# One output product per token tile, and a streamed input, between two layers of a hybrid mixer

## The chip, the cores and the metric

One core of a Trainium2 chip runs the whole program. The metric is the device time of one execution in microseconds (us). The engines that matter here are TensorE (PE, matrix products and transposes into PSUM, an on-chip memory of banks), VectorE (DVE), ScalarE (ACT), GpSimd (POOL) and SyncE (SP, whose queue issues most of the loads and stores). Each engine runs its instructions strictly in its own order and waits on semaphores for the others.

## What is computed

Two layers (`DEPTH = 2`) work on 256 latent and 256 context tokens of width 1024. Each layer normalises and modulates its input, multiplies it by one wide matrix, feeds three mixers (an RWKV-7 scan in both directions, a neighbourhood attention, a differential attention), merges their gated outputs, multiplies by `w_out`, normalises, and adds the result to its input:

```python
for l in range(DEPTH):
    mod_x = jax.nn.silu(c) @ w_mod[l] + b_mod[l]          # the same for the context
    sh_x, sc_x, gt_x = jnp.split(mod_x[:, None, :], 3, axis=-1)
    hx = _rmsnorm(x, g_pre[l]) * (1.0 + sc_x) + sh_x
    hcn = _rmsnorm(hc, g_pre[l]) * (1.0 + sc_c) + sh_c
    y_x, y_c = _mixer(hx, hcn, ...)                       # ends with ... @ w_out
    x = x + gt_x * _rmsnorm(y_x, g_post[l])
    if not last:
        hc = hc + gt_c * _rmsnorm(y_c, g_post[l])
return x
```

The last layer needs only the latent tokens' output, so its queries are 256 tokens, though its keys, values and RWKV states come from all 512.

## The kernel before

**Products.** Every fp32 product is split into three: each operand becomes a rounded high part and a low rest, and `mm3` (from line 250) issues high by high, high by low and low by high. `split` (from line 223) loads a 128x512 weight tile (`wr`, 256 KB, by SP), ACT copies it to `wh`, and DVE subtracts to get `wl`. There are 6, 5 and 4 buffers of these.

**The inverse.** `rwkv_inv` inverts four families of triangular 32x32 blocks for each RWKV segment, two segments per layer, so four times in all. DVE ends it with two stream transposes of the result, `RA` and `RB`. PE multiplies the off-diagonal blocks in two rounds, `QQ` and then `EE`. ACT empties the first round (`k<-a` in the trace), which the second reads, and copies the diagonal blocks of `RA` and `RB` into `Lab` (`Lab<-X`, four copies).

**The output product.** `outproj` works through four column blocks `c` of 256 and, in each, four weight tiles `kh`. With each weight tile it visits all token tiles `t` of 128 tokens (four in layer 0, two in layer 1). Two token tiles share one PSUM tile. After a block, ACT squares each tile's product with an accumulated sum, and DVE multiplies it by the gate into `y`. `ahead` is called with each weight tile and loads the residual's rows (`xt`) and the modulation weights (`wm`, 32 tiles for the next layer, the first 16 of them by the end of the product).

**The passage.** When the whole product is done, `residual` forms one reciprocal root for all token tiles (`rsqrt`: ten small DVE operations on 128 x tiles), and then adds the scaled product to each tile's residual rows. For the next layer, `start` then normalises all four tiles (`norm_rows`, two at a time: ACT squares, a `rsqrt`, then one half of each row scaled by ACT and one by DVE), PE transposes 32 blocks of 128x128 through a PSUM tile `b` of 512 columns, ACT copies each to SBUF, DVE modulates it with `mA` and `mB`, and `split_act` makes the high and low parts `h[0]`, `h[1]` that every product of the layer reads. The modulation vectors come from `mod_rows`: four groups `g` of 32 small matmuls into PSUM `y`, a row added by DVE, one PE transpose into `z`, and `mA` by DVE and `mB` by ACT. The first products of the new layer are the column blocks 6, 2 and 4 (over 512 tokens) and block 0 (256 tokens in layer 1). The gate blocks 7 and 8 (`gates`) follow later, woven between the RWKV steps by `weave`.

**What sets the order.** A scheduler places the instructions on each engine from the program's order and from priorities. `keep_in_program_order` pins a few of them. The buffers (52 slots `k` of 128x512, 2 stages `gs`, PSUM tags `z` 3, `a` 2, `b` 2, `y` 1) decide when a tile can be written again.

Of the kernel before, what the change touches and what calls it, by code (L numbers as in the profile page):

```python
# [20 lines left out]
NX = 256  # L21
T = 512
# [112 lines left out]
class K:  # L135
# [65 lines left out]
    def rsqrt(self, v, n, scale, eps, op=ALU.add, rows=128):  # L201

        a, b, y, t = (self.small(n) for _ in range(4))
# [158 lines left out]
    def mod_rows(self, l, P, ws):  # L362
# [86 lines left out]
    def start(self, l, P, xs, mod, ws, nr=T):  # L449

        self.in_order = l == 0
# [3 lines left out]
        for _ in range(8 if l == 0 else 0):  # L455
            next(mod)
# [29 lines left out]
        r = self.now(self.z_pair(l, 0, 0, nr))  # L486
        self.have["rx", l, 0] = True
        self.have["rz", l, 0] = row[0], self.rwkv_rows(l, P, 0, 1, r, 0, nr, nr == T) or [None, None], row[1]
# [288 lines left out]
    def rwkv_inv(self, e):  # L777
# [169 lines left out]
    def gates(self, l, n, b):  # L947

        for g in range(2):
# [322 lines left out]
    def outproj(self, l, s, ns, ss, ahead):  # L1272

        G = [self.gate_rows(l, st) for st in range(ns)]
        y = []
        for t in range(2 * ns):
            yt = self.k4.tile([128, 2, 512], F32, tag="k4", name=f"y{self.count()}")
            y.append([yt[:, 0, :], yt[:, 1, :]])
        for c in range(4):
            p = [self.ps("za"[c % 2], (128, 2, 256)) for _ in range(ns)]  # L1280
# [192 lines left out]
```

## Time and profile before

| | us |
|---|---|
| median of 3 runs | 1433.27 (1431.86 to 1433.6) |
| the profiled execution | 1431.83 |
| its span | 1430.0 |
| PE busy | 1314.2 (92%) |
| DVE busy | 973.4 (68%) |
| ACT busy | 811.5 (57%) |
| POOL busy | 234.6 (16%) |

The span is what the profiler sees from the first to the last instruction, and 1.83 us lie around it. The mean granted TensorE clock was 0.964 of full speed. In the rows below, `start, length, engine, line, operation, out<-in, shape, count` stand in a timeline, and the bracket at the end says how long the engine was idle just before and which instruction or transfer ended that. A line can be that of a helper: L195 is any matmul, L199 any transpose by PE, L164 any ACT operation, L185 any `tensor_tensor`, L167 any load or store.

### The profile page before, as it was taken

Reading aid. Unit: us, or ns where it says so; the run is one execution under the profiler, and the core shown is the slowest. Engines: PE = TensorE matmul, PEld = TensorE weight load, DVE = VectorE, ACT = ScalarE, POOL = GpSimd, SP = SyncE. Lnnn points to the kernel's source line nnn. Section 1 sums busy time; section 2 is a strip of 40 time slices with the busy share of each in tenths; the row PEclk is TensorE's granted clock in tenths of the full one; section 3 lists DMA queues with packets and bytes.
Section 4 is the critical chain, followed back from the end, with each engine's and each line's share of the span. In section 5 each row is a group of like instructions: output and inputs, shape, how many; then the busy total and the mean of one; then the engine's idle time right before and its main releaser. Section 6 shows DMA issues by size and latency. Waiting matters only on the chain. (4 is left out here: it accounts for less than half of the span.)

```text
span 1430.0 us, 28585 instructions
## 1 busy us (share of the span) xinstructions
PE 1314.2 (92%) x10784; PEld 1097.1 (77%) x10784; DVE 973.4 (68%) x2047; ACT 811.5 (57%) x1750; POOL 234.6 (16%) x292
## 2 busy tenths in 40 slices
PE   6998999899998999999899969998999999989796
PEld 4865777788777876677778958887888789867686
DVE  4763469726887367768675367768837892689886
ACT  5462375545964436667533355766558736567653
POOL 0010011003110012223235001011111000022441
PEclk9999999999998999999999989999989999999998
DMA  9466642324314268422533943553613242685454
GB/s 357 125 202 191 201 137 81 118 77 143 124 62 124 64 172 236 150 97 81 199 127 122 315 156 107 186 173 115 188 61 97 75 140 69 196 266 169 130 163 148
DMA packets 112986, 212.42 MB, mean 149 GB/s; under 512 B 13088, under 2 KB 24880, under 8 KB 112848
## 3 DMA queue, kind: packets, MB, share of 16 engines
q1 hardware_dynamic: 102896, 178.33, 39.4%
q0 software_dynamic: 9952, 32.26, 6.8%
q8 instruction: 85, 1.39, 0.4%
q14 instruction: 53, 0.43, 0.1%
HBM read 176.70 MB, written 33.83 MB: 147 GB/s over the span
## 5 line engine op out<-in xcount | busy, mean ns | idle before, releaser
L195 PE MATMUL z<-k,wh 128*128 128x512 f32 (+1 forms) x2288 | 633.5, 360 | 9.5 <-ACT wh L164 5.7
L195 PEld LDWEIGHTS z<-k,wh 128*128 128x128 f32 x2288 | 406.3, 194 | 75.7 <-issue 9.4
L195 PE MATMUL z<-k,wl 128*128 128x512 f32 (+1 forms) x1144 | 408.2, 359 | 8.6 <-DVE wl L185 8.6
L164 ACT ACTIVATE wh<-wr 128x512 fp32r<-128x512 f32 x376 | 234.2, 630 | 296.8 <-PE z L195 175.9
L185 DVE TENSOR_TENSOR wl<-wr,wh 128x512 fp32r<-128x512 f32 x376 | 280.3, 752 | 170.6 <-PE z L195 70.8
L195 PEld LDWEIGHTS z<-k,wl 128*128 128x128 f32 x1144 | 221.2, 194 | 41.8 <-DVE wl L185 12.8
L195 PE MATMUL z<-wh,k 128*128 128x256 f32 x704 | 140.3, 293 | 1.5 <-ACT k L164 1.3
L195 PEld LDWEIGHTS z<-wh,k 128*128 128x128 f32 x704 | 115.5, 198 | 3.5 <-ACT k L164 1.5
L185 POOL TENSOR_TENSOR k<-k,k 64x512 fp32r<-64x512 f32 (+3 forms) x64 | 78.4, 1231 | 168.5 <-ACT k L164 88.3
L195 PE MATMUL z<-wl,k 128*128 128x256 f32 x352 | 102.7, 292 | 1.6 <-DVE wl L185 1.5
L164 ACT ACTIVATE gs<-z 128x512 f32<-128x512 f32 (+1 forms) x132 | 66.1, 501 | 63.7 <-PE z L195 54.1
L164 ACT ACTIVATE k<-k 64x256 fp32r<-64x256 f32 (+5 forms) x154 | 79.4, 541 | 29.7 <-POOL k L185 21.8
L185 DVE TENSOR_TENSOR k<-k,k 128x256 f32<-128x256 f32 (+5 forms) x126 | 79.5, 644 | 17.8 <-ACT k L164 14.6
L199 PE MATMUL b<-cst,k 128*128 128x128 f32 x384 | 67.5, 292 | 21.0 <-ACT k L164 4.8
L199 PEld LDWEIGHTS b<-cst,k 128*128 128x128 f32 x384 | 45.2, 147 | 42.5 <-issue 14.0
L164 ACT ACTIVATE k<-a,s 128x512 f32<-128x512 f32 (+1 forms) x96 | 59.1, 616 | 32.5 <-DVE s L179 31.9
L164 ACT ACTIVATE k<-b 128x256 f32<-128x256 f32 (+1 forms) x152 | 67.3, 471 | 16.9 <-PE b L199 16.0
L195 PE MATMUL a<-k,k 128*128 128x512 f32 (+1 forms) x192 | 61.0, 399 | 12.5 <-ACT k L164 10.2
L195 PEld LDWEIGHTS z<-wl,k 128*128 128x128 f32 x352 | 69.6, 198 | 2.8 <-DVE wl L185 2.3
L195 PE MATMUL a<-ar,bk 64*128 64x128 f32 (+1 forms) x512 | 49.9, 285 | 10.0 <-ACT Lab L164 9.3
L195 PEld LDWEIGHTS a<-ar,bk 64*128 64x128 f32 x512 | 42.4, 187 | 21.7 <-ACT Lab L164 16.3
L179 DVE TENSOR_REDUCE s<-a 128x1 f32<-128x512 f32 (+1 forms) x96 | 56.4, 587 | 1.7 <-PE a L195 1.7
(169 smaller groups left out, 1948.8 us busy)
## 6 DMA issues: line engine op xcount, KB each, us to landing
wr<-in_wi SPq DMA_DIRECT2D x296, 256.0 KB, 3.0
k<-in_wm SPq DMA_DIRECT2D x64, 256.0 KB, 5.4
wr<-in_wb SPq DMA_DIRECT2D x48, 256.0 KB, 2.6
md<-gs SPq DMA_DIRECT2D x36, 256.0 KB, 2.7
k<-md POOLq DMA_DIRECT2D x36, 256.0 KB, 4.3
wr<-in_wg SPq DMA_DIRECT2D x32, 256.0 KB, 2.9
wr<-in_wo SPq DMA_DIRECT2D x32, 256.0 KB, 3.9
gd<-gs SPq DMA_DIRECT2D x18, 256.0 KB, 3.0
```

The source lines that it names most:

```text
L164: return self.nc.scalar.activation(out=out, in_=in_, func=func, **kw)
L179: return self.nc.vector.tensor_reduce(out=out, in_=in_, axis=AX.X, op=op, **kw)
L185: return (eng or self.nc.vector).tensor_tensor(out=out, in0=a, in1=b, op=op)
L195: return self.nc.tensor.matmul(out, lhsT=lhsT, rhs=rhs, start=start, stop=stop)
L199: return self.nc.tensor.transpose(out, in_, self.ident[0:k, 0:k])
```

## The change

- **Order of the output product.** In the last column block (`c == 3`) each token tile has a PSUM tile of its own, in different banks. The first token tile takes all four weight tiles as they come. The others follow one after the other, each over all four. As each is done, it is read, and `done` is called: for token tiles 0 and 1 it does the residual and the normalisation at once, each with its own `rsqrt`. Tiles 2 and 3 (the context) are kept in `late`.
- **Loads and modulation.** `ahead(i)` loads modulation tiles up to number 2i - 4 (before: i), and from the weight tile i = 7 on it steps `mod_rows` twice. So the modulation's matmuls stand between the weight tiles of the product, and the rest behind it.
- **The new layer's input.** `start` stays for layer 0. In its place layer 1 has `stream_in`: for each of 8 blocks two PE transposes into a PSUM tile (alternately `a` and `b`, so four banks), one ACT operation that modulates it on the way to SBUF, a DVE copy for the high part and a DVE subtraction for the low. It is done for the latent half first.
- **Order of the first products.** `start_next` takes block 0 for the latent half, the residual and normalisation of tiles 2 and 3, the two gate blocks (moved here from `zs`), the second half of the input, and then blocks 6, 2 and 4 over all 512 tokens.
- **The inverse.** The `QQ` matmuls are grouped by direction, the one that reads `RA` first. Two of the four diagonal copies go to DVE.
- **`rsqrt` for one column** has 8 operations, of which 4 take a scalar from SBUF, one per partition.

The diff, cut to its core:

```diff
+        if n == 1:
+            a, b, y, t = (self.small(1) for _ in range(4))
+            self.ts(a, v, scale, eps, ALU.mult, op)
+            self.ts(y.bitcast(I32), a.bitcast(I32), -0.5, float(0x5F3759DF), ALU.mult, ALU.add)
+            self.ts(t, y, y, a, ALU.mult, ALU.mult)
+            self.ts(b, t, -10.0 / 3.0, t, ALU.add, ALU.mult)
+            self.ts(y, b, 5.0, y, ALU.add, ALU.mult)
+            self.ts(t, y, y, a, ALU.mult, ALU.mult)
+            self.ts(t, t, -0.5 * 0.375 ** 3, 1.5 * 0.375, ALU.mult, ALU.add)
+            self.tt(y, t, y, ALU.mult)
+            return y
...
-                    ins = self.mm(mp[32 * i:32 * i + 32, g, :], self.cs[:, k].rearrange("p a b -> p (a b)"),
+                    self.mm(mp[32 * i:32 * i + 32, g, :], self.cs[:, k].rearrange("p a b -> p (a b)"),
                                   ws[8 * g + k][:, 128 * i:128 * i + 128], k == 0, k == 7)
-                    if l and g == k == i == 0:
-                        self.tc.keep_in_program_order(ins)
...
+    def stream_in(self, P, hn, s):
+        c = slice(256 * s, 256 * s + 256)
+        for k in range(8):
+            p = self.ps("ab"[k % 2], (128, 256))
+            self.turn_rows(hn, k, p)
+            t = self.slot((128, 256))
+            A, B = P["A"][:, s, k:k + 1], P["B"][:, s, k:k + 1]
+            self.act(t, p, AF.Identity, scale=A, bias=B)
+            self.cp(self.h[0][k][:, c], t)
+            self.tt(self.h[1][k][:, c], t, self.h[0][k][:, c].bitcast(F32), ALU.subtract)
+    def norm_row(self, x):
+        ss = self.small(2)
+        for j in range(2):
+            self.act(self.stage(512), x[j], AF.Square, accum_out=ss[:, j:j + 1])
+        s2 = self.small(1)
+        self.red(s2, ss, ALU.add)
+        rs = self.rsqrt(s2, 1, 1.0 / 1024, RMS_EPS)
+        self.act(x[0], x[0], AF.Copy, scale=rs)
+        self.ts(x[1], x[1], rs)
+    def start_next(self, l, P, nr, ctx):
+        r = self.now(self.z_pair(l, 0, 0, nr))
+        self.rwkv_rows(l, P, 0, 1, r, 0, nr, False)
+        ctx[0]()
+        self.now(self.gates(l, nr, 0))
+        ctx[1]()
+        self.rwkv_wa(l, P, self.now(self.z_pair(l, 6, 0, T)), 0, T)
+        row = [self.rwkv_rows(l, P, 0, w, self.now(self.z_pair(l, c, 0, T)), 0, T, True) for w, c in ((0, 2), (2, 4))]
+        self.have["rx", l, 0] = True
+        self.have["rz", l, 0] = row[0], [None, None], row[1]
...
+        def diag(d, q, copy):
+            R, r = RA if d == 0 else RB, rows(d, q)
+            copy(Lab[r, :, 32 * q:32 * q + 32], R[r].rearrange("p t k -> p k t"))
         for hf in range(2):
             QQ = self.ps("a", (128, 16, 32))
-            for k in range(16):
-                for d in range(2):
-                    rs, ra, cs = off(d)
-                    N = RB if d == 0 else RA
+            for d in (1, 0):
+                rs, ra, cs = off(d)
+                N = RB if d == 0 else RA
+                for k in range(16):
                     self.mm(QQ[ra, k, :], Lab[rs, 16 * hf + k, cs], N[rs, :, 16 * hf + k])
             q = self.slot((128, 16, 32))
+            self.act(q[64:96], QQ[64:96])
             self.act(q[32:64], QQ[32:64])
-            self.act(q[64:96], QQ[64:96])
             Qs.append(q)
+            diag(hf, 0, self.cp)
             yield self.yl[e["l"]]["q"][e["sg"]]
         for d in range(2):
-            R = RA if d == 0 else RB
-            for q in range(2):
-                r = rows(d, q)
-                self.act(
-                    Lab[r, :, 32 * q:32 * q + 32], R[r].rearrange("p t k -> p k t"))
+            diag(d, 1, self.act)
...
+            cs = slice(256 * (c % 2), 256 * (c % 2) + 256)
+            if c < 3:
+                pp = [self.ps("za"[c % 2], (128, 2, 256)) for _ in range(ns)]
+                p = [pp[t // 2][:, t % 2, :] for t in range(n)]
+            else:
+                p = [self.ps("aazz"[t], (128, 256)) for t in range(n)]
+            def part(w, kh, t):
+                for k in range(2):
+                    kk = 2 * kh + k
+                    self.mm3(p[t], [a[:, 128 * t:128 * t + 128] for a in s[kk]], [a[:, k, :] for a in w],
+                             kk == 0 and (c == 3 or t % 2 == 0), kk == 7 and (c == 3 or t % 2 == 1))
+            def read(t):
+                self.act(self.stage(256), p[t], AF.Square, accum_out=ss[t][:, c:c + 1])
+                self.tt(y[t][c // 2][:, cs], p[t], G[t // 2][c // 2][:, cs], ALU.mult)
+            ws = []
             for kh in range(4):
-                w = self.split(self.io["wo"][l, c, kh])
+                ws.append(self.split(self.io["wo"][l, c, kh]))
                 ahead(4 * c + kh)
-                for t in range(2 * ns):
-                    for k in range(2):
-                        kk = 2 * kh + k
-                        self.mm3(p[t // 2][:, t % 2, :], [a[:, 128 * t:128 * t + 128] for a in s[kk]],
-                                 [a[:, k, :] for a in w], kk == 0 and t % 2 == 0, kk == 7 and t % 2 == 1)
-            cs = slice(256 * (c % 2), 256 * (c % 2) + 256)
-            for t in range(2 * ns):
-                pt = p[t // 2][:, t % 2, :]
-                self.act(self.stage(256), pt, AF.Square, accum_out=ss[:, 4 * t + c:4 * t + c + 1])
-                self.tt(y[t][c // 2][:, cs], pt, G[t // 2][c // 2][:, cs], ALU.mult)
-        return y
+                for t in range(n if c < 3 else 1):
+                    part(ws[kh], kh, t)
+            for t in range(n):
+                if c == 3 and t:
+                    for kh in range(4):
+                        part(ws[kh], kh, t)
+                read(t)
+                if c == 3:
+                    done(t, y[t], ss[t])
...
-                    yield from self.gates(l, nq, 0)
+                    if l == 0:
+                        yield from self.gates(l, nq, 0)
...
+                    self.derived(l + 1, PN)
+                    self.h_new()
                     mod = self.mod_rows(l + 1, PN, ws)
                 def ahead(i):
                     if i % 4 == 3 and i // 4 < (2 if last else 4):
                         self.rows_load(xsrc, i // 4, xs)
-                    if not last and i >= 4:
-                        self.mod_load(l + 1, ws, i)
-                ss = self.small(8 if last else 16)
-                y = self.outproj(l, s, 1 if last else 2, ss, ahead)
+                    if not last:
+                        self.mod_load(l + 1, ws, 2 * i - 4)
+                        for _ in range(2 if i > 6 else 0):
+                            next(mod)
+                def rows(t, y, ss):
+                    self.residual(t, y, ss, xs[t], last)
+                    if not last:
+                        self.norm_row(xs[t])
+                def done(t, y, ss):
+                    if t < 2:
+                        rows(t, y, ss)
+                    else:
+                        late.append((t, y, ss))
+                self.outproj(l, s, 1 if last else 2, ahead, done)
                 if not last:
-                    next(mod)
-                self.residual(y, ss, xs, last)
-                if not last:
-                    self.start(l + 1, PN, xs, mod, ws, NX)
+                    self.mod_load(l + 1, ws, 32)
+                    self.now(mod)
+                    self.stream_in(PN, xs[0:2], 0)
+                    self.start_next(l + 1, PN, NX, (lambda: [rows(*a) for a in late],
+                                                    lambda: self.stream_in(PN, xs[2:4], 1)))
```

How the change moves instructions is shown at three places. A buffer's number is its name in the program, so that the same role has different numbers before and after.

**SP's queue around the last weight tile of the output product.** `in_wo` are the product's weights, `in_xt` the residual's rows, `in_wm` the modulation's weights, `in_wi` the next layer's. Before:

```order
L167 DMA k_9081<-in_wm 128x512
L167 DMA wr_9107<-in_wo 128x512
L167 DMA k_9113<-in_xt 128x512
L167 DMA k_9114<-in_xt 128x512
L167 DMA k_9117<-in_wm 128x512
L167 DMA k_9192<-in_wm 128x512
L167 DMA wr_9408<-in_wi 128x512
```

And now:

```order
L167 DMA k_9165<-in_wm 128x512
L167 DMA wr_9181<-in_wo 128x512
L167 DMA k_9187<-in_xt 128x512
L167 DMA k_9188<-in_xt 128x512
L167 DMA k_9191<-in_wm 128x512
L167 DMA k_9193<-in_wm 128x512
...
L167 DMA k_9384<-in_wm 128x512
L167 DMA wr_9522<-in_wi 128x512
```

Ten loads more stand ahead of the last `in_wo` tile, and 16 more ahead of the first `in_wi` tile (all 32 modulation tiles are now in front of it).

**ACT at the end of the product of layer 0.** `gs,s<-a` is the squared sum of a product tile, `gs,s<-k` that of normalised rows, `k<-k,s` the scaling of rows, and `k<-b` the copy of transposed blocks. Before:

```order
L164 ACTIVATE gs_9152,s_8560<-a_9010 128x256
L164 ACTIVATE mB_9159<-z_9353 128x2 x2
L164 ACTIVATE gs_9195,s_9194<-k_8671 128x512
L164 ACTIVATE gs_9197,s_9194<-k_8672 128x512
...
L164 ACTIVATE mB_9159<-z_9400 128x2 x2
L164 ACTIVATE k_8671<-k_8671,s_9207 128x512
...
L164 ACTIVATE k_9257<-b_9252 128x512
L164 ACTIVATE k_9264<-b_9259 128x512
```

And now:

```order
L164 ACTIVATE gs_9212,s_8599<-a_9105 128x256
L164 ACTIVATE mB_8871<-z_9200 128x2
L164 ACTIVATE wh_9524<-wr_9522 128x512
L164 ACTIVATE gs_9234,s_9233<-k_8705 128x512
L164 ACTIVATE gs_9236,s_9233<-k_8706 128x512
L164 ACTIVATE gs_9278,s_8600<-a_9106 128x256
L164 ACTIVATE wh_9536<-wr_9534 128x512
...
L164 ACTIVATE k_8705<-k_8705,s_9242 128x512
...
L164 ACTIVATE gs_9300,s_9299<-k_8859 128x512
...
L164 ACTIVATE k_9467<-a_9464,mB_8871,mA_8870 128x256
...
L164 ACTIVATE gs_9594<-z_9520,dv_948 128x256
...
L164 ACTIVATE gs_9619,s_9618<-k_9050 128x512
```

The squares of token tile 0 now stand behind the split of the next layer's first weight tile (`wh<-wr`), the squares of tile 2 (`k_9050`) behind the two readings of block 0's product (`gs<-z`), and the copy of transposed blocks has become the modulation with `mA` and `mB`.

**DVE at the first inverse.** `X` are the blocks and their transposes, `Lab` the matrix that the scan's steps read. Before:

```order
L185 TENSOR_TENSOR tmp_30_2456<-X_2359,X_2366 128x30
L185 TENSOR_TENSOR X_2366<-X_2366,tmp_30_2456 128x30
L182 STREAM_TRANSPOSE X_2809<-X_2366 128x1024
L182 STREAM_TRANSPOSE X_2810<-X_2366 128x1024
L185 TENSOR_TENSOR wl_2890<-wr_2887,wh_2889 128x512
```

And now:

```order
L185 TENSOR_TENSOR tmp_30_2456<-X_2359,X_2366 128x30
L185 TENSOR_TENSOR X_2366<-X_2366,tmp_30_2456 128x30
L182 STREAM_TRANSPOSE X_2809<-X_2366 128x1024
L182 STREAM_TRANSPOSE X_2810<-X_2366 128x1024
L176 COPY Lab_954<-X_2809 32x32x32
L176 COPY Lab_954<-X_2810 32x32x32
L185 TENSOR_TENSOR wl_2892<-wr_2889,wh_2891 128x512
```

Two copies into `Lab` now stand between the transposes and the next split of a weight tile, at this inverse and at the other three.

## Rows read from the trace of the kernel before

**Rows 1.** The page, section 1: busy time, share of the span, instructions.

```profile
PE 1314.2 (92%) x10784; PEld 1097.1 (77%) x10784; DVE 973.4 (68%) x2047; ACT 811.5 (57%) x1750; POOL 234.6 (16%) x292
```

**Rows 2.** The page's groups: busy us, mean ns of one, idle before it.

```profile
L185 DVE TENSOR_TENSOR wl<-wr,wh 128x512 fp32r<-128x512 f32 x376 | 280.3, 752 | 170.6 <-PE z L195 70.8
```

**Rows 3.** Timeline of SP's queue, 780 to 826 us: start, length, idle before.

```profile
786.63 0.91 SPq L167 DMA_DIRECT2D k<-in_xt  x2
...
805.89 0.33 SPq L167 DMA_DIRECT2D wr<-in_wo  x1
...
809.28 14.48 SPq L167 DMA_DIRECT2D wr<-in_wi  x10
```

**Rows 4.** Windows of 4 us: busy time by engine, PEclk, DMA share, GB/s.

```profile
808.00:812.00 4.00, 4.00 (x35) 4.00 (x35) 2.40 (x4) 2.15 (x6) 0.00 (x0) 1.00 1.06 386
```

**Rows 5.** Timeline of ACT, 808 to 850 us.

```profile
811.33 0.63 ACT L164 ACTIVATE wh<-wr 128x512 fp32r<-128x512 f32 x1 [0.71 <-DMA wr<-in_wo]
...
814.62 0.63 ACT L164 ACTIVATE wh<-wr 128x512 fp32r<-128x512 f32 x1 [0.97 <-DMA wr<-in_wi]
```

**Rows 6.** Timeline of PE, 818 to 850 us.

```profile
822.33 0.28 PE L195 MATMUL a<-wl,k 128*128 128x256 f32 x1
822.45 0.28 PE L195 MATMUL a<-wh,k 128*128 128x256 f32 x1
...
840.53 5.14 PE L199 MATMUL b<-cst,k 128*128 128x128 f32 x24 [0.47 <-ACT k L164]
846.92 0.73 PE L195 MATMUL z<-k,wh 128*128 128x512 f32 x2 [1.25 <-ACT k L164]
```

**Rows 7.** Windows of unequal length around the passage between the layers.

```profile
822.70:832.00 9.30, 4.13 (x130) 3.47 (x129) 8.45 (x26) 5.97 (x22) 2.18 (x4) 0.97 0.69 225
832.00:846.90 14.90, 8.30 (x33) 5.50 (x33) 8.13 (x38) 9.56 (x21) 0.54 (x1) 0.56 0.26 102
846.90:884.00 37.10, 37.08 (x274) 30.31 (x275) 22.08 (x53) 15.62 (x32) 1.08 (x2) 1.00 0.38 128
884.00:920.00 36.00, 33.42 (x243) 30.37 (x242) 31.41 (x67) 32.33 (x76) 6.41 (x12) 0.95 0.47 155
```

**Rows 8.** Timelines of PE at the four triangular inverses.

```profile
285.24 3.81 PE L195 MATMUL a<-X,k 32*32 32x32 f32 x128 [3.63 <-ACT k L164]
...
458.55 3.84 PE L195 MATMUL a<-X,Lab 32*32 32x32 f32 x128 [5.81 <-DVE X L182]
...
1030.46 3.80 PE L195 MATMUL a<-X,Lab 32*32 32x32 f32 x128 [1.62 <-DVE X L182]
...
1179.94 3.80 PE L195 MATMUL a<-X,Lab 32*32 32x32 f32 x128 [1.90 <-DVE X L182]
```

**Rows 9.** Timelines at the first and third inverse, ACT and then DVE.

```profile
272.69 8.11 ACT L164 ACTIVATE Lab<-X 32x1024 f32<-32x1024 f32 x4 [7.95 <-DVE X L182]
...
1027.19 3.12 DVE L182 STREAM_TRANSPOSE X<-X 128x1024 f32<-128x1024 f32 x2
```

**Rows 10.** Timelines of the program's end: ACT, DVE, SP's queue.

```profile
1420.05 0.38 ACT L164 ACTIVATE gs<-a 128x256 f32<-128x256 f32 x1 [4.32 <-PE a L195]
...
1421.86 0.15 DVE L179 TENSOR_REDUCE s<-s 128x2 f32<-128x8 f32 x1
...
1423.83 2.74 DVE L192 SCALAR_TENSOR_TENSOR k<-y,s,k 128x512 f32<-128x512 f32 x4
...
1424.60 2.32 SPq L167 DMA_DIRECT2D out_x<-k  x4
```

**Rows 11.** Groups by line and form: busy us, mean ns, idle before.

```profile
L176 DVE COPY k<-ar 64x256 f32<-64x256 f32 x24 | 7.6, 317 | 0.2
...
L185 DVE TENSOR_TENSOR k<-k,k 128x256 fp32r<-128x256 f32 x12 | 5.1, 463 | 0.0
...
L164 ACT ACTIVATE k<-b,dv 128x256 f32<-128x256 f32 x64 | 28.1, 471 | 8.2 <-PE b L195 6.5 <-PE z L195 1.1
...
L164 ACT ACTIVATE gs<-k 128x512 f32<-128x512 f32 x8 | 5.0, 631 | 1.5 <-DVE k L192 1.5
```

More of the change, by code (lines that the diff above doesn't have):

```diff
@@ L447, in h_new, with start @@
         self.h = ([self.slot(dt=F32R) for _ in range(8)], [self.slot(dt=F32R) for _ in range(8)])
-    def start(self, l, P, xs, mod, ws, nr=T):
-        self.in_order = l == 0
+    def stream_in(self, P, hn, s):
[27 more added lines that the diff above has]
+        self.have["rz", l, 0] = row[0], [None, None], row[1]
+    def start(self, l, P, xs, mod, ws):
+        self.in_order = True
         self.mod_load(l, ws, 16)
@@ L454, in start @@
         ht = []
-        for _ in range(8 if l == 0 else 0):
+        for _ in range(8):
             next(mod)
@@ L485, in start @@
         row = [self.rwkv_rows(l, P, 0, w, p[c], 0, T, True) for w, c in ((0, 2), (2, 4))]
-        r = self.now(self.z_pair(l, 0, 0, nr))
+        r = self.now(self.z_pair(l, 0, 0, T))
         self.have["rx", l, 0] = True
-        self.have["rz", l, 0] = row[0], self.rwkv_rows(l, P, 0, 1, r, 0, nr, nr == T) or [None, None], row[1]
+        self.have["rz", l, 0] = row[0], self.rwkv_rows(l, P, 0, 1, r, 0, T, True) or [None, None], row[1]
     def stage(self, n):
@@ L945, in gate_load, with gates @@
         return t
-    def gates(self, l, n, b):
-        for g in range(2):
+    def gates(self, l, n, b, gs=range(2)):
+        for g in gs:
             p = yield from self.z_pair(l, (7, 15, 23)[b] + g, 0, n)
@@ L1270, in merged, with outproj @@
         return s
-    def outproj(self, l, s, ns, ss, ahead):
+    def outproj(self, l, s, ns, ahead, done):
         G = [self.gate_rows(l, st) for st in range(ns)]
-        y = []
-        for t in range(2 * ns):
+        n = 2 * ns
+        y, ss = [], [self.small(4) for _ in range(n)]
+        for t in range(n):
             yt = self.k4.tile([128, 2, 512], F32, tag="k4", name=f"y{self.count()}")
@@ L1279, in outproj @@
         for c in range(4):
[L1280 removed]
+            cs = slice(256 * (c % 2), 256 * (c % 2) + 256)
[13 more added lines that the diff above has]
+            ws = []
             for kh in range(4):
[L1282 removed]
+                ws.append(self.split(self.io["wo"][l, c, kh]))
                 ahead(4 * c + kh)
[L1284 to L1294 removed]
+                for t in range(n if c < 3 else 1):
+                    part(ws[kh], kh, t)
+            for t in range(n):
+                if c == 3 and t:
[4 more added lines that the diff above has]
+                    done(t, y[t], ss[t])
     def rows_load(self, src, t, xs):
@@ L1299, in rows_load, with residual @@
         for j in range(2):
-            self.dma(self.nc.sync, xs[t][j], src[128 * t:128 * t + 128, 512 * j:512 * j + 512])
-    def residual(self, y, ss, xs, last):
-        n = len(y)
-        s2 = self.small(n)
-        self.red(s2, ss.rearrange("p (t j) -> p t j", j=4), ALU.add)
-        rs = self.rsqrt(s2, n, 1.0 / 1024, RMS_EPS)
-        for t in range(n):
-            for j in range(2):
-                rows = slice(128 * t, 128 * t + 128)
-                xo = xs[t][j]
-                self.stt(xo, y[t][j], rs[:, t:t + 1], xo, ALU.mult, ALU.add)
-                if last:
-                    self.dma(self.nc.sync, self.out[rows, 512 * j:512 * j + 512], xo)
-                elif t < 2:
-                    self.dma(self.nc.gpsimd, self.xd[rows, 512 * j:512 * j + 512], xo)
+            self.dma(self.nc.sync, xs[-1][j], src[128 * t:128 * t + 128, 512 * j:512 * j + 512])
+    def residual(self, t, y, ss, xs, last):
+        s2 = self.small(1)
+        self.red(s2, ss, ALU.add)
+        rs = self.rsqrt(s2, 1, 1.0 / 1024, RMS_EPS)
+        for j in range(2):
+            rows = slice(128 * t, 128 * t + 128)
+            xo = xs[j]
+            self.stt(xo, y[j], rs, xo, ALU.mult, ALU.add)
+            if last:
+                self.dma(self.nc.sync, self.out[rows, 512 * j:512 * j + 512], xo)
+            elif t < 2:
+                self.dma(self.nc.gpsimd, self.xd[rows, 512 * j:512 * j + 512], xo)
     def run(self):
@@ L1390, in run @@
                 xsrc = io["xt"] if l == 0 else self.xd
-                ws, xs = [], []
+                ws, xs, late = [], [], []
                 if not last:
+                    self.derived(l + 1, PN)
+                    self.h_new()
                     mod = self.mod_rows(l + 1, PN, ws)
```

1 line of the change is left out of this document (removed).

## The prediction

> **What bounds the kernel now.** I read the page's busy times first: PE works for 1314.2 of 1430.0 us [rows 1], so over the whole program the time is PE's work plus the gaps in it, and a change is worth the gaps it closes or opens. The second view is PE's timeline around the places that the diff touches, with the releaser of each gap. The third is windows around the passage between the layers. There PE is busy for 4.13 of 9.30 us and then 8.30 of 14.90 us [rows 7], the second stretch at a granted clock of 0.56, so mostly at the lower of the two levels (1.2 instead of 2.4 GHz) after the long gap before it. The last product matmul begins at 822.45 and the first matmul of layer 1 at 846.92 [rows 6]. Right after, 846.9 to 884 is full (37.08 of 37.10 us at clock 1.00), and 884 to 920 nearly so (33.42 of 36.00) [rows 7].
>
> **The inverse.** Four places. Before, the second round waited 3.63 us for ACT at the first inverse, and the first round waited 5.81, 1.62 and 1.90 us for DVE's transposes at the others [rows 8].
> - First inverse: four `Lab<-X` copies took 8.11 us of ACT ahead of the `k<-a` that the second round needs [rows 9], so 2.03 us each. Two of them go to DVE, 4.06 us less, and the 3.63 us of waiting vanish but for about 0.3 us, since other splits also stand in ACT's queue: -3.3.
> - The others: two transposes take 3.12 us, so 1.56 each [rows 9]. The direction that reads `RA` can start one transpose earlier. In the order of the second and third inverse, both its halves (32 matmuls, half of the 3.8 us of [rows 8]) come first and then cover the second transpose, so each saves about 1.5. At the fourth, only 16 stand in front (0.95 us of work against 1.56): -0.95, with perhaps -0.3 at its second round.
> - The sum is 3.3 + 1.5 + 1.5 + 1.25 = 7.5 us less. The two DVE copies (each 1.1 us if paced like the 317 ns copy of 256 elements [rows 11], 1.56 like the transpose at most) lie under the first round's 3.8 us, but the next weight split `wl` stands behind them. At worst, 3.1 us of copies and 0.75 us of split [rows 2] run 3.85 us after the transposes, about when the next `wl` is needed. Bounds: -8.5, or -3.5 if that cover is just too short at each.
>
> **The program's end.** Before, the last product ends, ACT squares token tile 0 at 1420.05, the reads of two tiles alternate to the reduction at 1421.86, ten small operations follow to 1423.83, and four residual operations (2.74 us, 0.69 each) feed four stores from 1424.60 [rows 10]. Now tile 0's part lies under tile 1's 24 matmuls (0.12 us apart [rows 6], so 2.9 us). Left behind the product are one read (about 0.95 us less), eight dependent operations for ten (about 0.2 each by 1421.86 to 1423.83, so -0.4; four of them now take their scalar from SBUF, which no row here prices on so small a tile: between nothing and another 0.2 us each, I take 0.1, so +0.4), and two residuals instead of four (-1.37): -2.3, with bounds -1.9 and -2.7.
>
> **The passage.** This is the uncertain term, and I walk it in order.
> - *Loads.* Before, 24 loads separate the issue at 786.63 from the last product weight's at 805.89, 0.8 us each, and that weight is split by ACT at 811.33 [rows 3, 5]. The queue is paced by bandwidth: from 808 to 812 us, the DMA engines were busy throughout at 386 GB/s [rows 4], so 0.68 us for 256 KB. Ten loads more in front make the last weight 6.8 to 8 us later: split at 818.1 to 819.3. The first weight of layer 1 has 16 more in front: split at 814.62 + 10.9 to 12.5, about 826 [rows 5].
> - *Product.* The third column block ends near 812. Tile 0's last part then waits for the weight and ends near 820.3, about 4 us of idle PE that were not there before. Tiles 1 to 3 follow with 2.9 us each, to about 829 (before 822.7, but with some 2 us of modulation still to come).
> - *The added wait.* The squares of tile 0 stand in ACT's queue behind the split of that first weight. They run at 826, not at about 823 when the residual is ready. Behind them are tile 1's read, the scaling and tile 1's squares (0.63 us and an accumulator read each [rows 11]). DVE's small chains of both tiles and four weight splits of 0.75 us interleave. Following the two queues row by row, tile 0 is scaled near 832, tile 1 near 840.7, and the first matmul of layer 1 comes near 842, 5 us earlier than before. PE idles there for about 10 us, slow clock included.
> - *First half.* Per block DVE copies and subtracts, 0.32 and 0.46 us; ACT needs 0.47 [rows 11] and hides. Eight blocks (6.2), two residuals of tile 2 (1.4), and four splits (3.0) make 10.6 us, to about 852.5. PE has 9.5 us of work there (block 0 and half a gate block, at 0.12 us a matmul, the pitch at the product's end [rows 6]), so about 1 us idle. The other gate work ends near 864, with 2.3 us of waiting for tile 2's transposes.
> - *Second half.* The norm of tiles 2 and 3 is one chain: DVE reaches tile 2's reduction only after the token shift of block 0 (four operations waiting for PE), near 854.4. Eight small operations among four splits, two residuals of tile 3, its squares, and eight more operations among four splits give tile 3's scale at about 869. Blocks 6, 2 and 4 start near 870, 6 us after PE ran dry. The first of them is paced by DVE, and the clock is low for a part of it: 2.5 us. All three end near 904 instead of 884.
>
> On the chain this is 20 us late, but block 0 and the gates (144 matmuls of 256 columns, 17 us) are already done. What counts is idle and slow time. Before: 5.17 + 6.60 of gaps, 4.9 of the 8.30 busy us lost to the clock (24 transposes took 5.14 us [rows 6], twice their time at full clock), and 2.58 plus up to 1.8 in 884 to 920 [rows 7]: about 21. After: 4 + 10 + 1 + 2.3 + 6 + 2.5 = 26. So +5. Bounds: -9 if the loads come at the faster pace and the chain of tiles 2 and 3 is hidden by the gates, +14 if that chain is 9 us longer.
>
> The Trainium skill bears on one price here: "VectorE: DVE Perf Modes", section "The perf-mode tier table", puts an fp32 copy between SBUF tiles in the 2x tier and keeps `tensor_tensor` at 1x. The nearest row shows 317 ns for 256 elements, which is no double rate, and I go by the row. By the page, a copy would be about 0.2 us (an estimate from its 1227 ns for 2048 elements), and the sum would be about 2 us lower over 16 copies.
>
> **The sum.** 1431.83 - 7.5 - 2.3 + 5 = 1427.0 for a profiled execution. That execution lies 1.44 under the median of the three runs (1433.27), so the median forecast is 1428.5.
>
> **The rivals.**
> - *The second half's chain is longer (slower).* Place: DVE and ACT between block 0's end and block 6's first matmul. Both are in-order queues in which weight splits wait for loads and for PE. At 8 to 9 us more, with block 6 starting near 879, the time is 1437. It decides from about 875, where the gain is used up. For it: DVE and ACT were already busy for 31.41 and 32.33 of 36 us in 884 to 920 [rows 7], and the chain crosses both four times. Against it: in the hole before, the same kind of chain ran without long waits.
> - *The holes close.* With the loads at 0.68 us, and the squares not held by the first weight, layer 1 starts near 836, and block 6 near 860, right behind the gates: 1431.83 - 7.5 - 2.3 - 5 + 1.44, so 1418.5. For it: the gates and block 0 are 17 us of PE work that need no context rows. Against it: the order of the queues that I walked.
> - *The inverse's gain is not kept.* PE arrives early, but the scan's next step waits for the same copies on ACT and DVE, or for a `wl` behind the copies. With half of the gain: 1432. For it: 5.81 us of waiting at the second inverse show that PE isn't always last there. Against it: ACT loses two copies at each.
>
> **How the numbers follow.** About 0.2% (2.9 us) can be told from no change, so faster means below 1430.4 and slower above 1436.1. The forecast with its own spread of some 4 us has 0.46 (0.38 faster, 0.08 same), the closing holes 0.18 (faster), the lost inverse 0.16 (0.13 same, 0.03 slower), and the longer chain 0.20 (slower). That makes faster 0.56, same 0.21, slower 0.23. The range takes in the closing holes and most of the longer chain: 1418 to 1438.5.
>
> **What would show it.** In the changed profile, the inverse's second round without its 3.63 us and the first rounds with about 1.5 us less; the last `wh<-wr` from `in_wo` of layer 0 near 819, the first from `in_wi` near 826; the first layer-1 matmul near 842; a gap of some 6 us ahead of block 6, near 864 to 870; one residual pair behind the last product matmul, and some 7.5 us from that to the span's end (before about 10). I'd be wrong if PE's gap after the product were as long as before, or if the first matmuls of block 6 came before 862 or after 878.

## The result

The changed kernel took 1442.49 us (median of 4 runs, 1439.05 to 1444.22) beside 1432.94 us for the kernel before. The ratio is 1.0069, with a 95% interval of 1.0047 to 1.0091: 6.7 to 13 us slower. The forecast was 1428.5 us, with a range up to 1438.5. The span of the profiled execution went from 1430.0 to 1440.5 us.

The page's busy times after (beside [rows 1]):

```profile
PE 1336.2 (93%) x10784; PEld 1115.8 (77%) x10784; DVE 985.8 (68%) x2109; ACT 794.0 (55%) x1742; POOL 234.9 (16%) x292
```

TensorE has as many instructions as before and is busy 22 us longer. So the loss is not one of gaps alone: matmuls that were there before take longer. The groups of TensorE by form (busy us, mean ns of one, idle before) show one that makes up 13.7 of the 22 us. After:

```profile
L195 PE MATMUL a<-X,Lab 32*32 32x32 f32 x512 | 28.9, 228 | 6.0 <-DVE X L182 5.9
...
L195 PE MATMUL a<-X,k 32*32 32x32 f32 x512 | 15.3, 229 | 0.0
```

And the first of the two before:

```profile
L195 PE MATMUL a<-X,Lab 32*32 32x32 f32 x512 | 15.2, 228 | 9.3 <-DVE X L182 9.3
```

`a<-X,Lab` is the first round of the inverse, `a<-X,k` the second. A matmul here leaves two records. One record takes 228 ns in either kernel, and in both the next begins before it ends. But 512 of them fill 28.9 us where they filled 15.2, so a new one begins about every 56 ns instead of every 30: fewer run side by side. PE's timeline after (beside [rows 8]) shows it place by place, and the second round at its old length:

```profile
275.59 6.75 PE L195 MATMUL a<-X,Lab 32*32 32x32 f32 x128
...
285.13 3.82 PE L195 MATMUL a<-X,k 32*32 32x32 f32 x128
...
459.80 3.83 PE L195 MATMUL a<-X,Lab 32*32 32x32 f32 x64 [5.01 <-DVE X L182]
...
464.71 3.81 PE L195 MATMUL a<-X,Lab 32*32 32x32 f32 x64
...
471.11 3.83 PE L195 MATMUL a<-X,k 32*32 32x32 f32 x128
...
1038.73 3.78 PE L195 MATMUL a<-X,Lab 32*32 32x32 f32 x64 [0.89 <-DVE X L182]
...
1043.59 3.81 PE L195 MATMUL a<-X,Lab 32*32 32x32 f32 x64
...
1050.19 3.82 PE L195 MATMUL a<-X,k 32*32 32x32 f32 x128
...
1188.48 6.89 PE L195 MATMUL a<-X,Lab 32*32 32x32 f32 x128
...
1200.63 3.80 PE L195 MATMUL a<-X,k 32*32 32x32 f32 x128
```

At the second and third inverse, 64 records take 3.8 us, as long as 128 did before; at the first and fourth, 128 take 6.75 and 6.89. From the first matmul of the first round to that of the second, the four inverses took 10.29, 6.84, 6.58 and 8.55 us before (the starts of both rounds in PE's timeline), and 9.54, 11.31, 11.46 and 12.15 after: 12.2 us more in sum. (Other matmuls stand between the rounds too, so this is a distance and not TensorE time alone.)

DVE's copies, on the other hand, cost about what was forecast (DVE at the third inverse, beside [rows 9]): 1.0 us each, and the split behind them comes in time. At none of the four inverses does PE's timeline show a wait for a `wl`.

```profile
1037.34 3.04 DVE L182 STREAM_TRANSPOSE X<-X 128x1024 f32<-128x1024 f32 x2
1040.30 2.03 DVE L176 COPY Lab<-X 32x1024 f32<-32x1024 f32 x2
1042.36 0.69 DVE L185 TENSOR_TENSOR wl<-wr,wh 128x512 fp32r<-128x512 f32 x1
```

The two profiles were lined up at three points of PE's timeline: the first matmul of layer 0's output product (773.67 before, then 778.92 after), the first round of the third inverse (1030.46 and 1038.73), and the last matmul's end (1419.95 and 1431.56).

```profile
773.67 0.28 PE L195 MATMUL z<-wh,k 128*128 128x256 f32 x1
...
778.92 0.28 PE L195 MATMUL z<-wh,k 128*128 128x256 f32 x1
```

This compares one execution of each kernel, and single executions scatter, as said below. The loss is 5.25 us when the product starts, 8.27 at the third inverse, 11.6 at the last matmul and 10.5 at the end. So the rebuilt passage, between the first two points, costs 3.0 us, and the program's end gains 1.1. The rest lies in the stretches with the inverses, and 4.6 us of that are given back between the third inverse's second round and the fourth's first (142.9 us before, 138.3 after). That stretch takes from 138.3 to 145.5 us in the eleven profiles of this document, so these 4.6 us may be scatter.

**The passage.** PE's timeline after (beside [rows 6]) shows a modulation transpose in the middle of the product, the modulation behind the product, the first matmul of layer 1, the last pieces of the gate blocks, and the first matmul of block 6:

```profile
821.28 0.33 PE L199 MATMUL z<-cst,k 128*128 128x128 f32 x1 [3.20 <-DVE k L185]
...
840.91 1.95 PE L195 MATMUL y<-k,cs 128*32 128x128 f32 x64
...
851.82 1.04 PE L195 MATMUL z<-k,wh 128*128 128x256 f32 x4
...
873.83 0.50 PE L195 MATMUL z<-k,wh 128*128 128x256 f32 x2 [2.62 <-DVE s L189]
...
879.96 0.79 PE L195 MATMUL z<-k,wh 128*128 128x512 f32 x1
```

SP's queue after (beside [rows 3]), with the last product weight and the first weights of layer 1:

```profile
818.34 0.33 SPq L167 DMA_DIRECT2D wr<-in_wo  x1
...
825.71 17.35 SPq L167 DMA_DIRECT2D wr<-in_wi  x10
```

And DVE, then ACT, around the transpose at 821.28 and the squares of tile 0:

```profile
820.33 0.69 DVE L185 TENSOR_TENSOR wl<-wr,wh 128x512 fp32r<-128x512 f32 x1 [1.34 <-ACT wh L164]
820.94 0.28 DVE L185 TENSOR_TENSOR k<-y,k 128x128 f32<-128x128 f32 x1
...
814.23 0.63 ACT L164 ACTIVATE wh<-wr 128x512 fp32r<-128x512 f32 x1 [7.92 <-DMA wr<-in_wo]
...
819.67 0.63 ACT L164 ACTIVATE wh<-wr 128x512 fp32r<-128x512 f32 x1 [1.40 <-DMA wr<-in_wo]
...
832.45 0.39 ACT L164 ACTIVATE gs<-a 128x256 f32<-128x256 f32 x1
...
836.20 0.63 ACT L164 ACTIVATE gs<-k 128x512 f32<-128x512 f32 x1 [2.69 <-DVE k L192]
```

The window that holds that wait, in the columns of [rows 4] (PE busy 2.80 of 6.00 us, PEclk 0.80):

```profile
818.00:824.00 6.00, 2.80 (x19) 2.22 (x19) 2.35 (x5) 1.85 (x4) 0.00 (x0) 0.80 1.04 378
```

**The end.** PE's last matmul, ACT's last read, and DVE's last operations (beside [rows 10]):

```profile
1431.28 0.28 PE L195 MATMUL a<-wh,k 128*128 128x256 f32 x1
...
1431.65 0.38 ACT L164 ACTIVATE gs<-a 128x256 f32<-128x256 f32 x1 [2.12 <-PE a L195]
...
1431.95 1.41 DVE L192 SCALAR_TENSOR_TENSOR k<-y,s,k 128x512 f32<-128x512 f32 x2
1433.29 0.42 DVE L185 TENSOR_TENSOR y<-a,k 128x256 f32<-128x256 f32 x1
...
1435.68 1.42 DVE L192 SCALAR_TENSOR_TENSOR k<-y,s,k 128x512 f32<-128x512 f32 x2
```

Tile 1's square is read at 1431.65, but its `y` is formed at 1433.29, because DVE is busy with tile 0's two residual operations from 1431.95. From the last matmul to the end of the span it took 8.9 us, and 10.05 before.

### The profile page after: what moved, and what is told of

It is laid out like the page before. It is cut to its first block, busy times and chain, and to the rows that moved or that the text cites. A ratio compares the mean times of both kernels' runs of the same rounds, so it can differ in the third digit from the quotient of the medians.

```text
span 1440.5 us, 28631 instructions
## 1 busy us (share of the span) xinstructions
PE 1336.2 (93%) x10784; PEld 1115.8 (77%) x10784; DVE 985.8 (68%) x2109; ACT 794.0 (55%) x1742; POOL 234.9 (16%) x292
## 4 chain that ended last, share of the span: by engine, by line
PE 59%; DVE 18%; ACT 10%; DMA 7%; issue 5%; POOL 1%; SPq 0%; DVEq 0%; ACTq 0%; POOLq 0%
PE z L195 36%; PE a L195 12%; ACT k L164 6%; PE y L195 5%; DVE wl L185 4%; DVE k L185 3%; PE b L195 3%; PE b L199 3%; DMA wr<-in_wi 2%; DVE k L192 2%; DMA k<-in_wm 2%; DVE X L182 2%; ACT wh L164 1%; DVE s L179 1%; DVE X L185 1%
## 5 line engine op out<-in xcount | busy, mean ns | idle before, releaser
L195 PE MATMUL z<-k,wh 128*128 128x512 f32 (+1 forms) x2352 | 653.4, 361 | 11.4 <-ACT wh L164 5.4
L195 PEld LDWEIGHTS z<-k,wh 128*128 128x128 f32 x2352 | 417.7, 194 | 80.6 <-issue 9.6
L195 PE MATMUL z<-k,wl 128*128 128x512 f32 (+1 forms) x1176 | 421.2, 360 | 9.0 <-DVE wl L185 8.9
L195 PEld LDWEIGHTS z<-k,wl 128*128 128x128 f32 x1176 | 226.8, 193 | 43.6 <-DVE wl L185 13.7
L195 PE MATMUL z<-wh,k 128*128 128x256 f32 x736 | 150.8, 300 | 1.6 <-ACT k L164 1.3
L195 PEld LDWEIGHTS z<-wh,k 128*128 128x128 f32 x736 | 124.7, 205 | 4.4 <-ACT k L164 1.5
L195 PE MATMUL z<-wl,k 128*128 128x256 f32 x368 | 109.7, 298 | 1.7 <-DVE wl L185 1.6
L185 DVE TENSOR_TENSOR k<-k,k 128x256 fp32r<-128x256 f32 (+5 forms) x134 | 80.8, 615 | 15.2 <-ACT k L164 11.6
L164 ACT ACTIVATE k<-k 64x256 fp32r<-64x256 f32 (+5 forms) x146 | 74.6, 537 | 29.3 <-POOL k L185 21.6
L195 PEld LDWEIGHTS z<-wl,k 128*128 128x128 f32 x368 | 75.3, 204 | 2.7 <-DVE wl L185 2.3
```

Of the source, the lines that this page charges most:

```text
L164: return self.nc.scalar.activation(out=out, in_=in_, func=func, **kw)
L185: return (eng or self.nc.vector).tensor_tensor(out=out, in0=a, in1=b, op=op)
L195: return self.nc.tensor.matmul(out, lhsT=lhsT, rhs=rhs, start=start, stop=stop)
```

## The experiments

Theory G: grouped matmuls of one direction use the same rows and columns of TensorE's array (a 32x32 part of it, by the shape 32*32 in the rows) and hold each other up, where those of alternating directions, on other rows and columns, run side by side. Its rival D: the two DVE copies stand in front of weight splits and hold the matmuls up. Against both stood the passage as the cause.

**The change with alternating matmuls.**

```diff
-            for d in (1, 0):
-                rs, ra, cs = off(d)
-                N = RB if d == 0 else RA
-                for k in range(16):
+            for k in range(16):
+                for d in range(2):
+                    rs, ra, cs = off(d)
+                    N = RB if d == 0 else RA
                     self.mm(QQ[ra, k, :], Lab[rs, 16 * hf + k, cs], N[rs, :, 16 * hf + k])
```

> The changed kernel with the first round of the inverse (QQ) alternating between the two directions again, as in the kernel before; the two diagonal copies stay on DVE and all else stays as changed. Theory G (grouping 16 matmuls of one direction makes them run one after the other, where alternating ones overlap: in the changed profile 64 records of a<-X,Lab take 3.83 us, in the profile of before 128 take 3.80): each first round falls from about 7.6 to 3.8 us, four times, so 15 us of TensorE work go; of them I expect 8 to 13 in the end, so 1430 to 1434 us. Rival D (the DVE copies ahead of the weight splits hold the matmuls up): within 2 us of the changed kernel, about 1441.

Measured: 1423.99 us, ratio to before 0.9935 (0.9914 to 0.9955). This edit is worth some 18 us and turns the loss into a gain. The first round's group is back at 15.3 us:

```profile
L195 PE MATMUL a<-X,Lab 32*32 32x32 f32 x512 | 15.3, 228 | 9.3 <-DVE X L182 9.3
```

Theory G holds, and by more than expected. Rival D falls.

**The kernel before with grouped matmuls.** The same edit the other way round, made in the kernel before.

> The kernel before with only the first round of the inverse grouped by direction, 16 matmuls each; all four diagonal copies stay on ACT. Theory G: the first rounds take 7.6 instead of 3.8 us and only some of it is given back by the earlier start, so 8 to 13 us slower, 1441 to 1446. Rival D: within 2 us of before, or up to 4 us faster by the earlier start.

Measured: 1443.06 us, ratio 1.0057 (1.0037 to 1.0077), 5 to 11 us slower. This edit alone costs as much as the whole change does:

```profile
L195 PE MATMUL a<-X,Lab 32*32 32x32 f32 x512 | 28.9, 229 | 6.0 <-DVE X L182 5.9
...
L195 PE MATMUL a<-X,k 32*32 32x32 f32 x512 | 15.3, 228 | 0.5 <-ACT k L164 0.5
```

The same regrouping costs some 18 us in the changed kernel and 5 to 11 here. The distances between the two rounds (their starts in PE's timelines) show the same difference: they add up to 44.5 us in the changed kernel and 25.4 in the first experiment, 19.1 apart, but to 43.5 here and 32.3 in the kernel before, 11.3 apart. In the kernel before, the second round waited for ACT anyway (3.63 us at the first inverse [rows 8]), and the longer first round fills most of that wait: 0.5 us is left in all. That is a part of the difference; the rest was not traced.

**The kernel before with the copies moved.**

```diff
+            diag(hf, 0, self.cp)
             yield self.yl[e["l"]]["q"][e["sg"]]
         for d in range(2):
-            for q in range(2):
-                self.act(Lab[r, :, 32 * q:32 * q + 32], ...)
+            diag(d, 1, self.act)
```

> The kernel before with only two of the four diagonal copies of the inverse moved from ACT to DVE (and the two readings of the first round swapped); the matmuls alternate as before. Theory G: the second round's 3.63 us of waiting at the first inverse goes, and little else: 2 to 4 us faster, 1429 to 1431. Rival D: 3 to 8 us slower, with gaps of TensorE at matmuls that wait for wl after the copies.

Measured: 1426.45 us, ratio 0.9949 (0.993 to 0.9969), 4 to 10 us faster, more than expected. PE's timeline at the four inverses, first and second round:

```profile
276.02 3.80 PE L195 MATMUL a<-X,Lab 32*32 32x32 f32 x128
...
282.60 3.80 PE L195 MATMUL a<-X,k 32*32 32x32 f32 x128
...
459.45 3.84 PE L195 MATMUL a<-X,Lab 32*32 32x32 f32 x128 [5.80 <-DVE X L182]
...
464.80 3.83 PE L195 MATMUL a<-X,k 32*32 32x32 f32 x128
...
1031.10 3.80 PE L195 MATMUL a<-X,Lab 32*32 32x32 f32 x128 [1.58 <-DVE X L182]
...
1036.40 3.83 PE L195 MATMUL a<-X,k 32*32 32x32 f32 x128
...
1176.97 3.85 PE L195 MATMUL a<-X,Lab 32*32 32x32 f32 x128 [2.30 <-DVE X L182]
...
1185.08 3.80 PE L195 MATMUL a<-X,k 32*32 32x32 f32 x128
```

The 3.63 us of waiting at the first inverse's second round [rows 8] are gone. The distances are 6.58, 5.35, 5.30 and 8.11 us, against 10.29, 6.84, 6.58 and 8.55 before, 6.9 us less in sum. At the second and third inverse, the second round had no gap in front of it before either, but other matmuls; now fewer of them stand there, and the round comes earlier on the scan's chain. How much of the gain comes from these two was not measured apart.

**The change with the whole old inverse.**

> The changed kernel with the whole inverse as in the kernel before, so the rebuilt passage, the product by token tiles and the short reciprocal root alone. By the two profiles the passage costs about 3 us (start of the output product 5.3 us late, next inverse 8.3 us late) and the end gains about 1.1 (8.9 instead of 10.0 us behind the last matmul): 1433 to 1436 us. If the passage were the cause of the loss: 1439 to 1443.

Measured: 1434.78 us, ratio 1.0012 (0.9996 to 1.0029), not to be told from before, and inside the forecast. The passage is not the cause of the loss: beside the changed kernel's 1.0069, the altered inverse costs some 8 us. In its profile the stretch from the product's first matmul to the third inverse takes 261.5 us, and 256.8 in the kernel before, and the end takes 8.6 us against 10.05.

The next four start from the kernel of the first experiment and look into the passage.

**With the old passage.** The output product of layer 0, `residual`, `start` and the place of the gates as before; inverse and end as changed.

> The kernel with alternating matmuls (first experiment, 1424.0) with the passage between the layers as in the kernel before (whole product, then residual, normalisation, transposes through one tile of 512 columns, blocks 6, 2, 4 and 0; gates woven in later); inverse with two DVE copies and the end by token tiles stay. Theory A (the costs add up: the passage costs the 3 us that the two profiles show between the start of the product and the third inverse): 1420 to 1422. Theory B (the passage gains once the inverse no longer delays the scan): what is left is the kernel with DVE copies (1426.5) and the shorter end (-1.1), so 1424 to 1427.

Measured: 1426.2 us, ratio 0.9951 (0.9932 to 0.9971). That is inside theory B's range, and even the lower end of the interval, 1423.3 us, is above theory A's. So theory A's time did not come about. Whether the kernel is faster with the old or with the new passage is not shown, since the interval overlaps that of the first experiment (0.9914 to 0.9955). The stretch from the product's first matmul to the third inverse still takes 258.3 us here and 261.7 with the new passage, in the first experiment's profile:

```profile
766.37 0.28 PE L195 MATMUL z<-wh,k 128*128 128x256 f32 x1
...
1028.09 3.80 PE L195 MATMUL a<-X,Lab 32*32 32x32 f32 x128 [1.62 <-DVE X L182]
```

Where the whole loses those 3.4 us again was not traced.

**Without the modulation in the product.**

```diff
-                        for _ in range(2 if i > 6 else 0):
-                            next(mod)
```

> The first experiment's kernel without stepping the modulation's matmuls between the weight tiles of the output product; they all stand behind it. The loads are asked for at the same places. Theory S (in the changed profile TensorE stood 3.20 us in front of a modulation transpose whose row waited in DVE's queue behind a weight split, at 821.28, and the clock fell to 0.80 there): the product ends 3 to 5 us earlier, and some 4 us of modulation move into the gap behind it, where TensorE waits anyway: 2 to 4 us less, 1420 to 1422. Rival (that stall only fills the wait for the last weight): within 1.5 us, 1422.5 to 1425.5, or slower where the modulation delays the first modulated block.

Measured: 1420.09 us, ratio 0.9909 (0.9884 to 0.9934). The stretch falls from 261.7 to 256.3 us. The product itself (first matmul's start to last one's end in PE's timeline) falls from 62.1 to 56.2 us, 5.9 us where 3 to 5 were expected.

**With 16 tiles ahead.**

```diff
-                        self.mod_load(l + 1, ws, 2 * i - 4)
+                        self.mod_load(l + 1, ws, min(2 * i - 4, 16))
```

> The first experiment's kernel with at most 16 modulation tiles asked for during the product (it uses no more there), the other 16 behind the last product weight. Ten loads fewer stand ahead of that weight. Theory L (the loads ahead hold the product up): the last weight is split 7 to 8 us earlier, the product ends 4 to 6 us earlier, and the time falls by 2 to 4 us, to 1420 to 1422. Rival: the first weight of layer 1 and the last modulation group come no earlier, so the gap behind the product grows by as much: within 1.5 us of 1424.

Measured: 1421.43 us, ratio 0.9918 (0.9895 to 0.9941). The stretch is 258.3 us. The last product weight is split 4.9 us earlier than in the first experiment, counted from the product's start, and the product ends 3.6 us earlier: both less than the 7 to 8 and 4 to 6 expected.

**Both.**

> Both edits: no modulation stepped in the product, and at most 16 of its tiles asked for during it. Theory S and L together: the product runs through as in the kernel before, and the time is 1418 to 1421. Rivals: within 2 us of 1424.

Measured: 1417.98 us, ratio 0.9893 (0.9874 to 0.9911), 13 to 18 us faster than before. The stretch is 254.2 us, 2.6 less than in the kernel before, and the product takes 51.0 us (49.1 in the kernel before). The interval of the ratio lies apart from those of the first experiment and of the old passage. Those of the two single edits overlap with the first experiment's, so neither is shown to gain alone. SP's queue in this kernel has the last four product weights in one run at 794.72, and six weights of layer 1 from 805.35, ahead of the last modulation tiles:

```profile
794.72 2.29 SPq L167 DMA_DIRECT2D wr<-in_wo  x4
...
805.35 3.72 SPq L167 DMA_DIRECT2D wr<-in_wi  x6
```

And PE's timeline has the modulation behind the product, one long wait for DVE's row there, and the first matmul of layer 1 at 833.20:

```profile
813.83 1.96 PE L195 MATMUL y<-k,cs 128*32 128x128 f32 x64
...
820.13 0.47 PE L199 MATMUL z<-cst,k 128*128 128x128 f32 x1 [3.25 <-DVE k L185]
...
833.20 0.48 PE L195 MATMUL z<-k,wh 128*128 128x256 f32 x2
```

**Which neighbours overlap.** The kernel before, grouped by direction, with consecutive matmuls from the two halves in turn:

```diff
+        for d in (1, 0):
+            rs, ra, cs = off(d)
+            N = RB if d == 0 else RA
+            for k in range(16):
+                for hf in range(2):
+                    self.mm(QQ[hf][ra, k, :], Lab[rs, 16 * hf + k, cs], N[rs, :, 16 * hf + k])
```

> The kernel before with the first round of the inverse grouped by direction as in the change, but with consecutive matmuls taken from its two halves in turn, so that neighbours write two different PSUM tiles while they use the same rows and columns of the array. One look at the length of the first round. Theory R (neighbours on the same rows and columns of the array can't overlap): 128 records of a<-X,Lab take 6.8 to 7.6 us, as when grouped. Rival W (neighbours that write the same PSUM tile can't overlap): about 3.8 us, as when the directions alternate.

Measured (one execution of each): 1443.23 us beside 1431.16.

```profile
L195 PE MATMUL a<-X,Lab 32*32 32x32 f32 x512 | 29.7, 229 | 6.0 <-DVE X L182 5.9
```

29.7 us for 512 records: a change of the PSUM tile from neighbour to neighbour wins nothing back, as long as they use the same rows and columns of the array. Theory W falls. Theory R holds in this sense: grouped records still begin before the last has ended, but at twice the distance. Whether the rows or the columns matter was not told apart, since the two directions differ in both.

## Why the prediction was wrong

- **The inverse's first round: the step that failed.** The prediction put "half of the 3.8 us" for 32 matmuls of one direction, so it took a rate measured on alternating directions for a grouped run. The runs showed 3.8 us for those 32 at the second and third inverse, twice the price, and 6.75 and 6.89 us for the whole first round at the others, where 3.8 were counted: 13.7 us more TensorE time (28.9 against 15.2). Undone, the time falls by 18 us. The term was forecast as -7.5. The timed runs with the new and the old inverse (1.0069 and 1.0012) put it at about +8, and the profiles agree: the distance between the rounds grew by 12.2 us, of which the earlier start of the first round gives back about 3 (5.01, 0.89 and no wait shown after, against 5.81, 1.62 and 1.90 [rows 8]). No rival covered this: the one on the inverse put its price at half the gain lost, not at a loss, and its reason was another.

  The Trainium skill states the rule under "TensorEngine Tiling (Array Packing)", section "Key Properties": different tiles of the array can load weights and multiply in parallel. The trace agrees: in 3.8 us run 128 records when neighbours use different tiles, and 64 when they use the same. It speaks against this edit, and it was not weighed.
- **The inverse's copies.** The mechanism was right and the size too small: -3.3 at the first inverse and about -0.3 elsewhere were credited to the two copies on DVE; alone, they bring the second rounds 6.9 us closer to the first in sum, and the kernel gains 4 to 10. The cover that was in doubt held. The copies took 1.0 us; the 1.1 of the prediction does not follow from the 317 ns row [rows 11] in proportion, which gives 1.27.
- **The passage.** Forecast +5; the stretch that holds it took 3.0 to 4.9 us longer in the three profiles that have it unaltered (259.8, 261.7 and 261.5 against 256.8; the other four profiles with the old passage have 256.9 to 258.3). The size came out near, but several steps were wrong and cancelled. Everything here is 5.25 us late, so that is taken off. The last weight was split at 818.4 (forecast 818.1 to 819.3), right. But tile 0's last part ended over 6 us later than the 820.3 forecast (ACT reads it at 832.45): PE stood idle for 3.20 us until 821.28, in front of a modulation transpose, whose row DVE had queued behind the split of a weight that had only just landed, while ACT had split the weights of the matmuls behind that transpose at 814.23. The added wait of the forecast, squares held by layer 1's first weight, did not come about: ACT was idle for 2.69 us and waited for DVE's residual, since tile 0 was so late. The first matmul of layer 1 came at 846.6 instead of 842, block 6 at 874.7 instead of 870. From there to the third inverse the time was 24.8 us shorter than before (158.8 for 183.5). The walk counted 17 us of work as already done there; the kernel before also had half of the modulation behind block 6 (128 records `y<-k,cs`, about 3.9 us at the 1.95 us for 64), and TensorE's idle time fell by 2.9 us. That the errors cancelled is luck.

  Two prices do not follow from their rows. Of 8.30 busy us at half the clock at most 4.15 are lost, not 4.9, so the sum before is about 20, not 21. And "no double rate" does not follow from the 317 ns of a small copy: the block copies took 0.29 us where subtractions of the same 256 elements took 0.43, and subtractions of 512 took 0.69 (DVE's timeline, 851.47, 851.80 and 820.33). By the two subtractions a fixed part of some 0.17 us is in each (an estimate), and less that, the copy takes about half the time of the subtraction. The 0.2 us that the prediction set against the row scales a large copy down in proportion, without such a fixed part.
- **The end.** Forecast -2.3, measured -1.1 and, in the six variants with the same end, -1.4 (8.6 to 8.7 us for 10.05). The term counted tile 0's part as hidden under tile 1's matmuls. Its two residual operations were not: DVE ran them ahead of tile 1's read, which waited 1.2 us for them.
- **The rivals.** The longer chain in the second half, the one rival with a slower end, was not it: from the first layer-1 matmul to block 6 it took 28.1 us, and 28 were forecast. The closed holes did not come about either: layer 1 began at 846.6, and that rival needed 836.

Three things stay open: whether the 4.6 us that the changed kernel gives back between the third and the fourth inverse are more than scatter, the whole effect of the new passage beside the old one, and a scatter between executions. Single profiles of kernels with the same code up to the output product begin it anywhere from 762.9 to 775.0 us (the first experiment and the four that start from it), so the 5.25 us at that point are not evidence of a loss, and spans of single executions were not compared for the verdicts, only timed ratios and stretches inside a profile.

The kernel with both edits, 1417.98 us, beats both the kernel before and the changed one.

## What to carry to other kernels

A rate read from a run of small matmuls holds only for their order: before regrouping matmuls on parts of the array, look at which parts the neighbours use, and at how far apart the records begin. The length of one record does not show it (228 ns in both orders); the busy time divided by the count does (30 and 56 ns). A transpose or a small matmul that is woven into a long product brings the queue of the engine that feeds it along, and everything behind it on TensorE waits for that queue. And a large diff should be priced edit by edit, since here a gain of 4 to 10 us and a loss of some 18 us stood in the same function.

## What the hardware showed unexpectedly

- 32 matmuls of 32x32 took 1.9 us when neighbours used different rows and columns of the array, and 3.8 us when they used the same (second and third inverse), whether or not they wrote the same PSUM tile.
- After the 3.20 us wait in the product, the granted clock of the window 818 to 824 was 0.80, and matmuls behind it began 0.22 us (822.50, 822.72) instead of 0.12 us apart (817.68, 817.80). The 24 matmuls behind the hole took 4.39 us (from 822.12), and 24 before it 3.13 (from 807.69): the hole cost 3.20 us and 1.26 more.
